# Expert bodies in another order with hinted jumps, and 20 weight rooms instead of 18

## The chip, the cores and the metric

The kernel runs on 1 core of one Trainium2 chip. The metric is the device time of one execution in microseconds; lower is better. TensorE is called PE below (its weight loads PEld), VectorE DVE, ScalarE ACT, GpSimd POOL, and SyncE SP.

## What is computed

A two-layer trunk over 256 latent tokens and 256 context tokens of width 1024: a layer with a convolution branch and a gating branch and a dense SwiGLU, then latent attention, and then the part that this case is about, a mixture of 8 experts of which each token takes 2:

```python
def _moe(h, router, w1, w3, w2):
    ...
    logits = (hf @ router).astype(jnp.float32)
    top_v, top_i = lax.top_k(logits, TOP_K)
    top_w = jax.nn.softmax(top_v, axis=-1)
    gates = jnp.sum(jax.nn.one_hot(top_i, N_EXPERTS, dtype=jnp.float32) * top_w[..., None], axis=-2).astype(h.dtype)
    y = jnp.zeros_like(hf)
    for e in range(N_EXPERTS):
        y = y + gates[:, e:e + 1] * _swiglu(hf, w1[e], w3[e], w2[e])
    return y.reshape(b, t, d)
```

All is float32. Expert width is 3584, so one expert has 3 x 1024 x 3584 weights, 44 MB, and the eight have 352 MB, which are read once.

## The kernel before

The first part (to about 768 us) runs the trunk up to the router. After it the kernel knows how many tokens each expert got. Tokens are handled in groups of 32, and an expert runs with 1, 2, 3 or 4 groups. This number is only known on the chip: line 1089 packs the eight numbers, two bits each (0 means one group, 2 means three), into one integer, which every engine reads into a register at line 1323. For each expert the program holds four bodies, one for each number of groups, and every engine branches to the one it needs:

```python
with tc.If(groups >= 2, preferred_fallthrough_block=True) as many:
    with tc.If(groups == 2, preferred_fallthrough_block=True) as three:
        body(3)
    with three.Else():
        body(4)
with many.Else():
    with tc.If(groups == 1, preferred_fallthrough_block=True) as two:
        body(2)
    with two.Else():
        body(1)
```

Code stands in the order of writing: the test for this expert, its bodies for 3, 4, 2 and 1 groups, then the test for the next expert. The block that stands right behind a test is reached without a jump; a body that is not the last one ends with a jump over those behind it.

A body (`expert`, line 1181) is seven steps j. In each, `up` (L1196) multiplies the gathered tokens with four rooms of weights, ACT and DVE form the SwiGLU (L1205, L1206), `turn` (L1212) transposes it, and `down` (L1225) multiplies it with two rooms, one step late. At the end `scale` (L1255) and `scatter` (L1266, L1270) add the result to the latents. Tokens are gathered for two experts at once: `hots` (L1113) makes a one-hot tile G, and `gather` (L1129, L1130) fills an operand tile xf, for the next pair at the end of the experts with odd number.

Weights come in pieces of 128 x 2048 floats, 1 MB, 42 to an expert, through a ring of 18 rooms: 6 from a pool of their own (`MORE`, tile names room), 4 and 8 that the trunk used before (roomsplit, raw). `ring.load()` (L172) is called when a room has been used and issues the load of the piece that is 18 pieces ahead; it stands on SP's queue and waits until PE has read the room. The order of instructions within PE, ACT and DVE is that of the code. The scratch tiles (line 265) come from a pool of six buffers that are handed out in turn.

Of the kernel before, what the change touches and what calls it, by code (L numbers as in the profile page):

```python
# [19 lines left out]
P = 128  # L20
# [18 lines left out]
MORE = 6  # L39
# [205 lines left out]
def trunk(ctx: ExitStack, tc, w, out, taps=None):  # L245
# [39 lines left out]
    right = ExitStack()  # L285
    xp = right.enter_context(tc.tile_pool(name="xp", bufs=1, side="right"))
# [86 lines left out]
    class Sum:  # L373


        def __init__(self, n):
            self.n, self.acc, self.last = n, None, None

        def square(self, ap):
            if self.acc is None:  # L380
                self.acc = small.tile([P, T], F32, tag="sum", name="sum", bufs=2)[:, : self.n]
                nc.scalar.activation(self.acc, ap, AF.Square)
            else:
                if self.last is not None:
                    nc.vector.tensor_add(self.acc, self.acc, self.last)
                self.last = scratch()[:, : self.n]
                nc.scalar.activation(self.last, ap, AF.Square)
# [84 lines left out]
    st = Sum(T)  # L472
# [23 lines left out]
    with tc.tile_pool(name="mix", bufs=1, side="right", reuse_waits="tile") as mix:  # L496
# [181 lines left out]
        st = Sum(T)  # L678
# [26 lines left out]
        var = Sum(T)  # L705
# [43 lines left out]
    with tc.tile_pool(name="ffn", bufs=1, side="right", reuse_waits="tile") as fp:  # L749
# [11 lines left out]
        st = Sum(T)  # L761
# [50 lines left out]
    with tc.tile_pool(name="latent", bufs=1, side="left", reuse_waits="tile") as lt:  # L812
        kvl = lt.tile([P, 2, T], F32, name="kvl")
        ql = lt.tile([P, 3, TX], F32, name="ql")
        skv, sq = Sum(T), Sum(TX)
# [182 lines left out]
    st = Sum(TX)  # L998
# [108 lines left out]
    with tc.tile_pool(name="exp", bufs=1, side="right", reuse_waits="tile") as ep:  # L1107
# [3 lines left out]
        def hots(p):  # L1111
            G = ep.tile([P, 2, 2, CAP], F32R, tag="G", name="G")
# [4 lines left out]
        def operand_room():  # L1117
            return ep.tile([P, KD, 2, CAP], F32, tag="xf", name="xf", bufs=2)

        def gather(p, ks, kind):  # L1120

            if p not in xfs:
                xfs[p] = operand_room()
# [57 lines left out]
        def expert(e, s):  # L1181
# [27 lines left out]
            def turn(h):  # L1209
# [3 lines left out]
                ht = ep.tile([P, 512], F32, tag="ht", name="ht", bufs=2)  # L1213
# [37 lines left out]
            def scale():  # L1251
                y = ep.tile([P, N_GROUPS, 2 * P], F32, tag="y", name="y")
                for b in range(nb):
                    n = min(2, s - 2 * b)
                    nc.vector.tensor_mul(y[:, 2 * b : 2 * b + n, :], state["y"][b][:, :n, :],  # L1255
                                         gate_row.unsqueeze(1).to_broadcast([P, n, 2 * P]))
                return y

            def scatter(y):
                back = state["back"]  # L1260
                accs = [bank("BC"[t % 2]) for t in range(4)]
                for t in range(2):
                    for g in range(s):
                        for q in range(4):
                            row = slice(32 * q, 32 * q + 32)
                            nc.tensor.matmul(accs[q][:, t * TX : (t + 1) * TX], back[row, g, t * P : (t + 1) * P], y[row, g, :],  # L1266
# [6 lines left out]
            for j in range(N_J):  # L1273
# [20 lines left out]
            y = scale()  # L1294
            if after:
                gather(after, range(4, KD), "A")
            scatter(y)
# [16 lines left out]

        hots(0)
        tokens(0, (1,))
# [36 lines left out]
        def overflow():  # L1353

            G = ep.tile([P, 2, 2, CAP], F32, tag="G", name="G")[:, 0]
            GT = ep.tile([P, N_GROUPS, TX], F32, tag="back", name="back")[:, 0, :]
            y = ep.tile([P, N_GROUPS, 2 * P], F32, tag="y", name="y").rearrange("p g n -> p (g n)")
            ht = ep.tile([P, 512], F32, tag="ht", name="ht", bufs=2)
# [191 lines left out]
```

## Time and profile before

| | |
|---|---|
| runs, us | 1744.45, 1745.65, 1749.63 (median 1745.65) |
| profiled execution: its time | 1745.33 us |
| profiled execution: its span | 1743.5 us |
[...]
| busy: PE, DVE, ACT | 1628.2, 510.4, 388.7 us |
| data moved | 470.40 MB |

The span is the time from the first to the last instruction of one profiled execution. Busy time of PE is the time in which at least one of its pipelined matmuls was under way. The profile's other views are: the chain of waits (from the last instruction back, at each step to what released it), the timeline (instructions in order of time, with the idle time before them and what ended it), the stretches (busy time of each engine, granted clock and share of the 16 DMA engines in a given window) and the waits (who waited for whom).

### The profile page before, as it was taken

How to read it: one execution, taken by the hardware profiler on the slowest of the kernel's cores; microseconds unless marked ns; L12 is line 12 of the kernel's file. 1: busy time of each engine (PE TensorE's matmuls, PEld its weight loads, DVE VectorE, ACT ScalarE, POOL GpSimd, SP SyncE). 2: the span in 40 equal slices, each digit the busy share in tenths (PEclk: the TensorE clock that was granted, in tenths of full speed). 3: DMA queues.
4: the chain of work that ended last, by engine and by line, in shares of the span. 5: the costliest groups of instructions: out<-in, count | busy, mean ns of one | idle time of the engine just before them, and what ended most of it. 6: DMA issues, size and time to landing. Idle time of an engine off the chain costs nothing.

```text
span 1743.5 us, 40718 instructions
## 1 busy us (share of the span) xinstructions
PE 1628.2 (93%) x18697; PEld 1109.3 (64%) x18697; DVE 510.4 (29%) x929; ACT 388.7 (22%) x724; POOL 23.1 (1%) x20
## 2 busy tenths in 40 slices
PE   8998999999999999999967799989999967998996
PEld 5676678888888787876533455555665533555654
DVE  3899763333433667720010000010010010100001
ACT  4343452222223355632000100000100001000101
POOL 0022000000000000000000000000000000000000
PEclk9999999999999999999988899999999987999998
DMA  9652562222222544689969999969979969999970
GB/s 379 225 233 73 242 242 97 94 88 97 91 79 97 200 187 176 232 325 354 394 247 421 419 419 351 298 250 367 399 295 379 377 259 420 419 419 418 418 287 28
DMA packets 67332, 470.40 MB, mean 270 GB/s; under 512 B 7456, under 2 KB 7840, under 8 KB 13088
## 3 DMA queue, kind: packets, MB, share of 16 engines
q1 hardware_dynamic: 67104, 467.13, 69.0%
q8 instruction: 171, 2.80, 0.7%
q14 instruction: 57, 0.47, 0.1%
HBM read 466.05 MB, written 1.05 MB: 268 GB/s over the span
## 4 chain that ended last, share of the span: by engine, by line
PE 83%; DMA 9%; DVE 3%; issue 3%; ACT 1%; SPq 0%; ACTq 0%; DVEq 0%
PE bankA L1196 28%; PE bankB L1225 13%; PE bankA L270 7%; PE bankA L271 7%; PE bankA L272 7%; DMA raw<-e 6%; PE bankB L271 3%; PE bankB L270 3%; PE bankB L272 3%; DVE cv L524 2%; PE bankC L339 2%; DMA room<-e 2%; PE bankC L1212 1%; DMA roomsplit<-e 1%; PE bankA L339 1%
## 5 line engine op out<-in xcount | busy, mean ns | idle before, releaser
L1206 DVE TENSOR_TENSOR scratch<-scratch,bankA 128x256 f32<-128x256 f32 (+1 forms) x98 | 31.9, 353 | 783.3 <-ACT scratch L1205 783.3
L1196 PE MATMUL bankA<-raw,xf 128*32 128x256 f32 x3888 | 231.5, 392 | 28.4 <-issue 16.9
L1196 PEld LDWEIGHTS bankA<-raw,xf 128*32 128x32 f32 x3888 | 130.3, 113 | 115.7 <-issue 32.3
L1196 PE MATMUL bankA<-room,xf 128*32 128x256 f32 x3264 | 190.1, 388 | 9.8 <-issue 4.9
L132 DVE TENSOR_TENSOR split<-raw,split 128x1024 fp32r<-128x1024 f32 (+4 forms) x121 | 139.9, 1158 | 113.3 <-ACT split L131 111.0
L1205 ACT ACTIVATE scratch<-bankA 128x256 f32<-128x256 f32 (+1 forms) x98 | 32.2, 330 | 597.5 <-PE bankA L1196 595.8
L131 ACT CAST split<-raw 128x1024 fp32r<-128x1024 f32 (+4 forms) x121 | 118.0, 980 | 199.5 <-PE bankA L272 121.3
L1196 PEld LDWEIGHTS bankA<-room,xf 128*32 128x32 f32 x3264 | 106.3, 112 | 85.0 <-issue 12.4
L1196 PE MATMUL bankA<-roomsplit,xf 128*32 128x256 f32 x2256 | 132.3, 392 | 23.9 <-issue 21.2
L270 PE MATMUL bankA<-hq,split 128*128 128x512 f32 (+1 forms) x380 | 148.7, 392 | 1.4 <-ACT hq L450 1.4
L271 PE MATMUL bankA<-hq,split 128*128 128x512 f32 (+1 forms) x380 | 148.2, 390 | 0.9 <-DVE hq L453 0.9
L272 PE MATMUL bankA<-hq,split 128*128 128x512 f32 (+1 forms) x380 | 147.3, 388 | 0.0
L1225 PE MATMUL bankB<-raw,ht 128*32 128x256 f32 x2288 | 135.2, 388 | 7.5 <-DMA raw<-e 5.5
L1196 PEld LDWEIGHTS bankA<-roomsplit,xf 128*32 128x32 f32 x2256 | 75.9, 113 | 77.0 <-issue 27.4
L1225 PEld LDWEIGHTS bankB<-raw,ht 128*32 128x32 f32 x2288 | 74.3, 112 | 61.3 <-DMA raw<-e 6.7
L1225 PE MATMUL bankB<-room,ht 128*32 128x256 f32 x1632 | 92.9, 382 | 6.1 <-DMA room<-e 4.9
L524 DVE SCALAR_TENSOR_TENSOR cv<-pad,prm,cv 128x512 f32<-128x512 f32 x106 | 86.0, 848 | 0.8
L270 PEld LDWEIGHTS bankA<-hq,split 128*128 128x128 f32 x380 | 71.6, 189 | 21.9 <-issue 3.4
L271 PEld LDWEIGHTS bankA<-hq,split 128*128 128x128 f32 x380 | 71.7, 189 | 16.2 <-DVE hq L453 1.4
L272 PEld LDWEIGHTS bankA<-hq,split 128*128 128x128 f32 x380 | 71.6, 188 | 14.5
L1225 PEld LDWEIGHTS bankB<-room,ht 128*32 128x32 f32 x1632 | 52.8, 110 | 42.8 <-DMA room<-e 3.6
L1214 ACT COPY ht<-bankC 128x384 f32<-128x384 f32 (+2 forms) x56 | 24.6, 439 | 242.3 <-PE bankC L1212 242.3
(403 smaller groups left out, 2028.3 us busy)
## 6 DMA issues: line engine op xcount, KB each, us to landing
raw<-e SPq DMA_DIRECT2D x146, 1024.0 KB, 10.4
room<-e SPq DMA_DIRECT2D x114, 1024.0 KB, 11.5
roomsplit<-e SPq DMA_DIRECT2D x72, 1024.0 KB, 9.4
raw<-ada SPq DMA_DIRECT2D x48, 1024.0 KB, 7.6
raw<-f SPq DMA_DIRECT2D x26, 1024.0 KB, 5.2
raw<-f SPq DMA_DIRECT2D x8, 896.0 KB, 4.7
raw<-win SPq DMA_DIRECT2D x6, 1024.0 KB, 7.7
raw<-wout SPq DMA_DIRECT2D x4, 1024.0 KB, 8.4
```

The lines of the kernel that those rows point to most:

```text
L131: self.nc.scalar.copy(wh[:, :size], raw)
L132: self.nc.vector.tensor_sub(wl[:, :size], raw, wh[:, :size].bitcast(F32))
L270: nc.tensor.matmul(acc, wh, ah, start=first, stop=False)
L271: nc.tensor.matmul(acc, wh, al, start=False, stop=False)
L272: nc.tensor.matmul(acc, wl, ah, start=False, stop=last)
L339: nc.tensor.matmul(acc[32 * q : 32 * q + 32, :], cs[:, 4 * h + q, :], wt[:, q, :], start=(h == 0), stop=(h == 1), tile_position=(0, 32 * q))
L524: nc.vector.scalar_tensor_tensor(out=o, in0=i, scalar=cw[:, m, j : j + 1], in1=o, op0=ALU.mult, op1=ALU.add)
L1196: nc.tensor.matmul(accs[g // 2][32 * q : 32 * q + 32, g % 2], xf[:, k, g * GROUP : (g + 1) * GROUP], piece[:, k - kk, :, q * P : (q + 1) * ...
L1205: nc.scalar.activation(part, acc[:, :n, 0, :], AF.Silu)
L1206: nc.vector.tensor_mul(part, part, acc[:, :n, 1, :])
L1214: nc.scalar.copy(ht[:, : s * P], tp[:, : s * P])
L1225: nc.tensor.matmul(state["y"][g // 2][32 * t : 32 * t + 32, g % 2], ht[:, g * P + f * GROUP : g * P + (f + 1) * GROUP], piece[:, f - ff, t ...
```

## The change

There are three parts.

The order of the bodies: the first test is now whether the expert has other than three groups, and the code stands in the order test, bodies for 1, 4, 2 and 3 groups, next test. A body for 1, 4 or 2 groups ends with a jump, that for 3 groups runs into the next test. At the start of each body, PE gets a hint instruction that names the next expert's first test and, from the packed number, whether it will jump (0, three groups) or not (1). One such hint, with a fixed direction, stands ahead of the first expert. Only PE has hints, and only the first test of each expert is named by one.

The rooms: `MORE` is 8 instead of 6, so the ring has 20 rooms.

The space for them: the operand tile xf exists once instead of twice; G, ht and y are taken from the scratch tiles, y as one or two tiles; G is made right ahead of the gather instead of in step 3; the row of final gains has a tile of its own; and the tiles in which squares are summed move from a pool that lives throughout to pools of the stages.

```diff
-MORE = 6
+MORE = 8
...
     right = ExitStack()
+    sums_of = right.enter_context(tc.tile_pool(name="sums", bufs=2, side="right"))
...
-                self.acc = small.tile([P, T], F32, tag="sum", name="sum", bufs=2)[:, : self.n]
+                self.acc = self.pool.tile([P, self.n], F32, tag=f"sum{self.n}", name="sum", bufs=1 if self.n < T else 2)
...
         def hots(p):
-            G = ep.tile([P, 2, 2, CAP], F32R, tag="G", name="G")
+            G = scratch(F32R).rearrange("p (t i s) -> p t i s", t=2, i=2)
...
         def operand_room():
-            return ep.tile([P, KD, 2, CAP], F32, tag="xf", name="xf", bufs=2)
+            return ep.tile([P, KD, 2, CAP], F32, tag="xf", name="xf")
...
-                ht = ep.tile([P, 512], F32, tag="ht", name="ht", bufs=2)
+                ht = scratch()
...
             def scale():
-                y = ep.tile([P, N_GROUPS, 2 * P], F32, tag="y", name="y")
-                for b in range(nb):
+                ys = [scratch().rearrange("p (g n) -> p g n", g=2) for _ in range(nb)]
+                for b, y in enumerate(ys):
...
-                if j == 3 and after:
-                    hots(after)
...
             if after:
+                hots(after)
                 gather(after, range(4), "A")
...
+        xfs[0] = operand_room()
         hots(0)
+        tc.mark_branch_hint_location("groups0", engines={mybir.EngineType.PE})
...
-            if e == N_EXP - 2:
-                fg_row = operand_room().rearrange("p k i s -> p (k i s)")[:, :D]
             if e % 2 and e + 1 < N_EXP:
-                xfs[e // 2 + 1] = operand_room()
+                xfs[e // 2 + 1] = xfs[0]
+            if e == N_EXP - 1:
+                fg_row = ep.tile([P, D], F32, name="fg_row")
...
                 with ordered():
+                    if e + 1 < N_EXP:
+                        tc.mark_branch_hint_location(f"groups{e + 1}", hint=(packed // 4 ** (e + 1)) % 4 != 2,
+                                                     engines={mybir.EngineType.PE})
                     expert(e, s)
 
-            with tc.If(groups >= 2, preferred_fallthrough_block=True) as many:
-                with tc.If(groups == 2, preferred_fallthrough_block=True) as three:
-                    body(3)
-                with three.Else():
-                    body(4)
-            with many.Else():
-                with tc.If(groups == 1, preferred_fallthrough_block=True) as two:
-                    body(2)
-                with two.Else():
+            with tc.If(groups != 2, preferred_fallthrough_block=True, label=f"groups{e}") as other:
+                with tc.If(groups == 0, preferred_fallthrough_block=True) as one:
                     body(1)
+                with one.Else():
+                    with tc.If(groups == 3, preferred_fallthrough_block=True) as four:
+                        body(4)
+                    with four.Else():
+                        body(2)
+            with other.Else():
+                body(3)
```

PE's order in the built program, at the entry to the first expert. Before, both tests are followed by the body for three groups (24 matmuls to a room, 8 to a group):

```order
L1323 TENSOR_LOAD classes
L1339 REGISTER_ALU
L1339 COMPARE_AND_BRANCH
L1340 REGISTER_ALU
L1340 COMPARE_AND_BRANCH
L1196 MATMUL bankA<-room_5418,xf 32x256 x24
L1196 MATMUL bankA<-room_5420,xf 32x256 x24
```

Now:

```order
L1322 TENSOR_LOAD classes
L1341 REGISTER_ALU
L1341 COMPARE_AND_BRANCH
L1342 REGISTER_ALU
L1342 COMPARE_AND_BRANCH
L1337 ISA
L1337 REGISTER_ALU
L1546 BRANCH_PREFETCH_HINT
L1195 MATMUL bankA<-room_5422,xf 32x256 x8
L1195 MATMUL bankA<-room_5424,xf 32x256 x8
```

The body for one group now follows the tests, with a hint and two register instructions at its start; the body for three groups has moved to the end.

PE's order where the first expert's last body ends and the second expert begins. Before, that last body is the one for one group, and the one for three groups follows the second expert's tests:

```order
L1266 MATMUL bankC<-y,back 128x256
L1345 UNCONDITIONAL_BRANCH
L1339 ISA
L1339 COMPARE_AND_BRANCH
L1340 REGISTER_ALU x2
L1340 COMPARE_AND_BRANCH
L1196 MATMUL bankA<-raw_5453,xf 32x256 x24
```

Now the last body is the one for three groups:

```order
L1264 MATMUL bankC<-scratch,back 128x256
L1341 UNCONDITIONAL_BRANCH
L1341 ISA
L1341 COMPARE_AND_BRANCH
L1342 REGISTER_ALU x2
L1342 COMPARE_AND_BRANCH
L1337 ISA
L1337 REGISTER_ALU
L1546 BRANCH_PREFETCH_HINT
L1195 MATMUL bankA<-room_5426,xf 32x256 x8
```

An expert with three groups now runs straight into a next expert with one group, as one with one group ran into one with three before. The branch at the end of the last body leads to the row behind it.

## Rows read from the trace of the kernel before

**Rows 1.** The page's head.
```profile
span 1743.5 us, 40718 instructions
```

**Rows 2.** Chain of waits, second to fourth expert: start us, us, what, with matmul records.
```profile
915.66 3.59 PE bankA L1196 x64
...
999.99 13.95 PE bankA L1196 x256
...
1161.68 10.50 PE bankA L1196 x192
1172.18 5.18 PE bankB L1225 x96
1177.36 0.48 PE bankC L1212 x3
```

**Rows 3.** Waits of SP's queue: line, releaser, us in total, times, longest.
```profile
SPq L172 <- PE bankA L1196: 343.6, 143, 13.6
```

**Rows 4.** Timeline of PE, first up of each expert: start, us, work, [idle before <-releaser].
```profile
768.58 10.57 PE L1196 MATMUL bankA<-room,xf 128*32 128x256 f32 x192 [0.69 <-issue]
903.88 5.03 PE L1196 MATMUL bankA<-raw,xf 128*32 128x256 f32 x64 [14.08 <-issue]
980.86 4.49 PE L1196 MATMUL bankA<-roomsplit,xf 128*32 128x256 f32 x39 [5.70 <-issue]
1145.62 1.07 PE L1196 MATMUL bankA<-room,xf 128*32 128x256 f32 x4 [3.17 <-issue]
1274.57 12.25 PE L1196 MATMUL bankA<-raw,xf 128*32 128x256 f32 x192 [2.81 <-issue]
1409.72 5.35 PE L1196 MATMUL bankA<-roomsplit,xf 128*32 128x256 f32 x48 [14.26 <-issue]
1480.73 10.57 PE L1196 MATMUL bankA<-room,xf 128*32 128x256 f32 x192
1605.33 0.23 PEld L1196 LDWEIGHTS bankA<-raw,xf 128*32 128x32 f32 x8 [5.78 <-issue]
1605.36 13.04 PE L1196 MATMUL bankA<-raw,xf 128*32 128x256 f32 x192 [5.41 <-DMA roomsplit<-e]
```

**Rows 5.** DMA queues from 889 to 904 us: packets, MB, share of 16 engines.
```profile
q8 instruction: 5, 0.08, 3.2%
```

**Rows 6.** Stretches: length, PE PEld DVE ACT POOL busy, PEclk, DMA share, GB/s.
```profile
1140.00:1160.00 20.00, 15.77 (x232) 8.57 (x226) 2.48 (x4) 0.00 (x0) 0.00 (x0) 0.83 0.42 155
1500.00:1520.00 20.00, 20.00 (x371) 11.89 (x365) 1.54 (x5) 1.80 (x5) 0.00 (x0) 1.00 1.01 419
1680.00:1700.00 20.00, 20.00 (x367) 11.91 (x363) 1.26 (x4) 1.80 (x5) 0.00 (x0) 1.00 0.36 134
```

**Rows 7.** The same in stretches of 5 us, first to second expert.
```profile
890.00:895.00 5.00, 0.00 (x0) 0.00 (x0) 1.98 (x4) 0.00 (x0) 0.00 (x0) 0.81 0.37 146
895.00:900.00 5.00, 0.00 (x0) 0.00 (x0) 0.00 (x0) 0.00 (x0) 0.00 (x0) 0.50 0.04 8
900.00:905.00 5.00, 1.12 (x12) 0.69 (x16) 0.00 (x0) 0.00 (x0) 0.00 (x0) 0.50 0.04 7
905.00:910.00 5.00, 4.16 (x57) 2.14 (x49) 0.29 (x1) 0.28 (x1) 0.00 (x0) 0.83 0.60 195
```

**Rows 8.** The same, fifth to sixth expert.
```profile
1395.00:1400.00 5.00, 0.47 (x8) 0.06 (x2) 2.48 (x4) 0.00 (x0) 0.00 (x0) 0.82 0.48 192
1400.00:1405.00 5.00, 0.00 (x0) 0.00 (x0) 0.00 (x0) 0.00 (x0) 0.00 (x0) 0.50 0.05 8
1405.00:1410.00 5.00, 0.28 (x4) 0.23 (x8) 0.00 (x0) 0.00 (x0) 0.00 (x0) 0.50 0.04 7
1410.00:1415.00 5.00, 5.00 (x52) 2.65 (x48) 0.00 (x0) 0.00 (x0) 0.00 (x0) 0.50 0.48 136
```

**Rows 9.** Instructions that use G: durations ns min/median/max, first and last start.
```profile
L1113 DVE TENSOR_TENSOR G<-cst,pos x4: 683/684/691, 756.9 to 1432.8; 128x512 fp32r<-128x512 f32 x4
```

More of the change, by code (lines that the diff above doesn't have):

```diff
@@ L373, in trunk, with __init__ @@
     class Sum:
-        def __init__(self, n):
-            self.n, self.acc, self.last = n, None, None
+        def __init__(self, n, pool):
+            self.n, self.pool, self.acc, self.last = n, pool, None, None
         def square(self, ap):
             if self.acc is None:
-                self.acc = small.tile([P, T], F32, tag="sum", name="sum", bufs=2)[:, : self.n]
+                self.acc = self.pool.tile([P, self.n], F32, tag=f"sum{self.n}", name="sum", bufs=1 if self.n < T else 2)
                 nc.scalar.activation(self.acc, ap, AF.Square)
@@ L471, in trunk @@
     warm(13)
-    st = Sum(T)
+    st = Sum(T, sums_of)
     for k in range(KD):
@@ L677, in trunk @@
         ready_for(AF.Sqrt, u[:, 3, :])
-        st = Sum(T)
+        st = Sum(T, sums_of)
         def mix_out(h):
@@ L704, in trunk @@
             nc.tensor.matmul(mean, mean_w, cv[:, m, :], start=(m == 0), stop=(m == 3))
-        var = Sum(T)
+        var = Sum(T, sums_of)
         for m in range(4):
@@ L759, in act @@
             return s
-        st = Sum(T)
+        st = Sum(T, sums_of)
         for t in range(3):
@@ L814, in trunk @@
         ql = lt.tile([P, 3, TX], F32, name="ql")
-        skv, sq = Sum(T), Sum(TX)
+        skv, sq = Sum(T, lt), Sum(TX, lt)
         for m, acc in outer([f"owkv{m}" for m in range(3)], hi, lo):
@@ L997, in trunk @@
     raw_lg = bank("C")
-    st = Sum(TX)
+    st = Sum(TX, rp)
     ready_for(AF.Sqrt, o)
@@ L1117, in operand_room @@
         def operand_room():
-            return ep.tile([P, KD, 2, CAP], F32, tag="xf", name="xf", bufs=2)
+            return ep.tile([P, KD, 2, CAP], F32, tag="xf", name="xf")
         def gather(p, ks, kind):
-            if p not in xfs:
-                xfs[p] = operand_room()
             for k in ks:
@@ L1251, in scale, with scatter @@
             def scale():
-                y = ep.tile([P, N_GROUPS, 2 * P], F32, tag="y", name="y")
-                for b in range(nb):
+                ys = [scratch().rearrange("p (g n) -> p g n", g=2) for _ in range(nb)]
+                for b, y in enumerate(ys):
                     n = min(2, s - 2 * b)
[L1255 to L1259, printed above, removed]
+                    nc.vector.tensor_mul(y[:, :n, :], state["y"][b][:, :n, :], gate_row.unsqueeze(1).to_broadcast([P, n, 2 * P]))
+                return ys
+            def scatter(ys):
                 back = state["back"]
@@ L1265, in scatter @@
                             row = slice(32 * q, 32 * q + 32)
-                            nc.tensor.matmul(accs[q][:, t * TX : (t + 1) * TX], back[row, g, t * P : (t + 1) * P], y[row, g, :],
+                            nc.tensor.matmul(accs[q][:, t * TX : (t + 1) * TX], back[row, g, t * P : (t + 1) * P], ys[g // 2][row, g % 2, :],
                                              start=(t == 0 and g == 0), stop=(t == 1 and g == s - 1), tile_position=(32 * q, 0))
@@ L1291, in expert @@
             if after:
+                hots(after)
                 gather(after, range(4), "A")
             down(N_J - 1, ht)
-            y = scale()
+            ys = scale()
             if after:
                 gather(after, range(4, KD), "A")
-            scatter(y)
+            scatter(ys)
         def final_norm():
@@ L1353, in overflow @@
         def overflow():
-            G = ep.tile([P, 2, 2, CAP], F32, tag="G", name="G")[:, 0]
+            G = scratch().rearrange("p (i t s) -> p i t s", i=2, t=2)[:, 0]
             GT = ep.tile([P, N_GROUPS, TX], F32, tag="back", name="back")[:, 0, :]
-            y = ep.tile([P, N_GROUPS, 2 * P], F32, tag="y", name="y").rearrange("p g n -> p (g n)")
-            ht = ep.tile([P, 512], F32, tag="ht", name="ht", bufs=2)
+            y, ht = ep.tile([P, KD, 2, CAP], F32, tag="xf", name="xf").rearrange("p k i s -> p (k i s)")[:, :D], scratch()
             rooms, row, xe = ring.rooms[: ROOMS], ring.rooms[ROOMS][:, :D], ring.rooms[ROOMS + 1][:, :D]
```

## Prediction

> **What bounds the kernel now.** I read the page's head first: the profiled execution spans 1743.5 us [rows 1]; its own time is 1745.33 us, 1.8 more, and the median of the three runs is 1745.65, so a sum made against the profile carries over unchanged. Then the chain of waits, from 768 us on, where the experts begin: each expert is an alternation of up, turn and down, and its number of groups can be read from the matmul records of one up, 64 per group: 64 records in 3.59 us, 192 in 10.50, 256 in 13.95 [rows 2]. Read so, the eight experts e0 to e7 run with 3, 1, 4, 3, 3, 1, 3, 3 groups. Each needs 42 rooms of 1 MB. Where the transfers are saturated they move 419 GB/s [rows 6], so a room takes 1.0486 MB / 0.419 = 2.50 us, and one j of six rooms 15.0 us. PE needs for the same j 10.50 + 5.18 + 0.48 = 16.2 us with three groups and more with four; with one group an up takes 3.59 us for four rooms, 0.9 each. So experts of 3 and 4 groups are bound by PE, and the ring of 18 rooms stands full ahead of them; e1 and e5, with one group, eat the ring up and are then bound by the transfers. The queue confirms it: the loads of line 172 wait 343.6 us for a room that PE frees [rows 3].
>
> Third, the timeline at the change from one expert to the next. I name the gap in PE between the last scatter and the first up, and how many jumps PE makes there by the old order of the bodies (test, 3, 4, 2, 1 groups, next test): e0-e1 three jumps (out of body 3, to the second test, to body 1), 14.08 us; e1-e2 one (to body 4), 5.70; e2-e3 one, 3.17; e3-e4 one, 2.81; e4-e5 three, 14.26; e5-e6 none, and the up starts with no gap at all; e6-e7 one, 5.41, which PE's weight loads put to "issue" [rows 4]. The chain lays that last wait to a DMA, but the room had landed long before: the transfers run ahead of PE there and end by 1690 [rows 6]. So a jump has a price, and rows give it: one jump 2.8 to 3.2 us where the transfers pause, 5.4 to 5.7 where they are saturated, and each further jump in a row (14.2 - 3.0) / 2 = **5.6 us** (the first is cheaper because scatter's matmuls are still queued ahead of it). During a gap the code queue moves 16 KB packets, 5 of them between 889 and 904 us [rows 5], so the wait is for code.
>
> [...]
>
> **Two of the gaps stop the transfers too.** In e0-e1 PE frees no room for 14 us. The ring is full, and the DMA share falls to 0.37, 0.04, 0.04, 0.60 [rows 7]: idle (0.63 + 0.96 + 0.96 + 0.40) x 5 = 14.8 us. In e4-e5 likewise: (0.52 + 0.95 + 0.96 + 0.52) x 5 = 14.8 us [rows 8]. As e1 and e5 end when their last room lands, these 15 us each are on the path.
>
> **The change, transition by transition.** The new order of the bodies is test, 1, 4, 2, 3 groups, next test. A jump to body 3 now carries a hint from the body before; all other jumps carry none.
>
> - Into e0: before, body 3 follows the test (a gap of 0.69 us [rows 4]); now a hinted jump. Bounds 0 and 5.6; I take +0.5, close to the 0.69 of the entry without a jump, since the hint stands at the program's start.
> - e0-e1 and e4-e5: no jump any more (body 3, next test, body 1 stand in a row, as e5-e6 does now with no gap). The transfers still pause until PE has freed its first room (0.9 us of a one-group up) and the queue has issued: about 1 us. That leaves -13.8 for each.
> - Two more rooms: at the ends of e0 and e4 the ring is full, so two more rooms of e1 and e5 lie ready, 2 x 2.50 = -5.0 each. The DMA share is 0.42 around e2-e3 [rows 6], so there is time to fill them. In the other experts they are worth nothing, as PE is the bound.
> - e1-e2: two jumps without a hint instead of one (body 1 to the next test, test to body 4). The second costs 5.6, or 8.2 if saturated transfers add the same 2.6 as they do to a single jump (5.41 - 2.81). I take +8.2, since the transfers are saturated there.
> - e2-e3: one jump as before, then a hinted one straight behind it. Bounds 0 and 5.6; the hint has only the few instructions of the test to work in. I take +3.
> - e3-e4: only a hinted jump, reached by falling through. 2.81 + 1.7 goes, 0.5 stays for the tests: -4.0. Bounds -4.5 and 0.
> - e5-e6: before no jump; now an unhinted one (5.5, saturated), a hinted one right behind (0 to 8.2, I take 5), and the slow first up (2.5): +13, bounds +8 and +16.2. PE is the bound from there to the end, so all of it counts.
> - e6-e7: only a hinted jump: 5.41 + 2.5 - 0.5 = -7.4, bounds -7.9 and 0.
>
> Everything else I cost at nothing. G is now made right ahead of its use: 0.68 us on DVE [rows 9], while PE does a down; in e1 and e5, where PE waits for rooms, this is free, and if the cover were gone it would be 0.7 us three times. One operand tile instead of two: its next contents are written after the last up that reads it. Shared scratch: six buffers, and each comes round again after three uses of the pair h, ht, when its reader is long done. The sums move to other pools ahead of the experts with their orders unchanged. Two more loads stand on SP's queue behind all weights of the trunk. ACT, DVE and SP jump without hints too: ACT and DVE have the next expert's first up (10.5 us and more before a three- or four-group body) as cover, SP the loads that are already queued. The three instructions for a hint at a body's start are hidden behind scatter where PE falls through.
>
> Sum, in the order of the experts: +0.5 - 18.8 + 8.2 + 3 - 4.0 - 18.8 + 13 - 7.4 = **-24.3**, so 1745.33 - 24.3 = **1721 us**.
>
> [...] The rows show code coming in 16 KB packets, and PE standing still for 14 us while a handful of them move [rows 5]. [...]
>
> **The rivals.**
>
> 1. The hints do nothing (the change doesn't do all it says). Each jump to body 3 then costs what an unhinted one does: +5.6 into e0, +5.6 at e2-e3, 0 at e3-e4 and e6-e7, +16.2 at e5-e6. Sum: 5.6 - 18.8 + 8.2 + 5.6 + 0 - 18.8 + 16.2 + 0 = -2.0, or 1743. For it: no row shows a hint at work. Against: only that the program names branch and direction well ahead. Chance 0.16.
> 2. The hints work even right behind another jump: nothing into e0, nothing at e2-e3, +8 at e5-e6, and 5.6 instead of 8.2 at e1-e2. Sum: 0 - 18.8 + 5.6 + 0 - 4.0 - 18.8 + 8 - 7.4 = -35.4, or 1710. Chance 0.08.
> 3. The rooms bring nothing, or the hinted jumps out of a fall-through hide only in part (the test may stand early in its code block): up to 10 us of the gain go, 1729 to 1739. Against the first: the idle transfers in rows 7 and 8 say that the ring was full. Chance 0.12.
> 4. Slower: a hint at a body's start makes PE fetch the far block at once and drop the code that it needs next, so that each of the seven bodies with a hint stalls at its start. At a price p the sum is -24.3 + 7p; it is slower than before by over 0.3% once p passes 4.2 us. At the 5.6 of a chained jump it is +14.9, or 1760. Nothing in the trace speaks for it, and the price of a jump is above the point, so it can't be excluded. Chance 0.06.
>
> The forecast itself, 1713 to 1729, has 0.58.
>
> **How the numbers follow.** About 0.3%, 5.2 us, is what a measurement here can tell from no change. Faster by more (below 1740.4): 0.58 + 0.08 + 0.12, and a third of rival 1 (0.06), 0.84. Same: the rest of rival 1, 0.10. Slower: 0.06. Range 1708 to 1743: it leaves out half of rival 2 (0.04), half of rival 1 (0.08) and rival 4 (0.06).
>
> **What would show it.** Right: the two gaps of 14 us gone, the first up of e1 and e5 within 1 us of the scatter, and the DMA share near 1 through both; e1 and e5 done about 19 us sooner after the scatter before them; gaps of under 1 us at e3-e4 and e6-e7; gaps of some 12 to 14 us at e1-e2, 6 at e2-e3 and 10 at e5-e6. Wrong: gaps of 3 to 5 us still at e3-e4 and e6-e7 (the hints do nothing), gaps at a body's start behind its first instructions (rival 4), or a pause of the transfers of over 3 us at e0-e1 (some other engine or the queue jumps late).

## The result, and the profile of the changed kernel

The changed kernel takes 1718.22 us, the median of four runs (1716.95 to 1720.21), against 1746.78 us for the kernel before (four runs, 1744.45 to 1749.63): a ratio of 0.9837, with an interval of 0.9818 to 0.9855. The forecast was 1721 us. The profiled execution is the longest of the four, 1720.21 us; its span, from the head of the page of after, answers to [rows 1]:

```profile
span 1718.4 us, 40666 instructions
```

The timeline of PE in the changed kernel, first up of each expert, answers to [rows 4] (start, us, work, idle time before it in brackets; up is line 1195 now). A new line begins where the room's name changes or where PE waited inside the up; behind such a wait the second piece has a bracket too.

```profile
769.24 12.25 PE L1195 MATMUL bankA<-room,xf 128*32 128x256 f32 x192 [1.03 <-issue]
...
891.94 3.66 PE L1195 MATMUL bankA<-room,xf 128*32 128x256 f32 x64
...
970.36 1.46 PE L1195 MATMUL bankA<-room,xf 128*32 128x256 f32 x9 [13.50 <-issue]
975.49 16.48 PE L1195 MATMUL bankA<-room,xf 128*32 128x256 f32 x247 [3.67 <-issue]
...
1141.74 7.09 PE L1195 MATMUL bankA<-room,xf 128*32 128x256 f32 x96 [5.96 <-issue]
1148.64 5.37 PE L1195 MATMUL bankA<-raw,xf 128*32 128x256 f32 x96
...
1265.09 10.57 PE L1195 MATMUL bankA<-raw,xf 128*32 128x256 f32 x192
...
1384.25 2.80 PE L1195 MATMUL bankA<-raw,xf 128*32 128x256 f32 x48
...
1460.05 4.08 PE L1195 MATMUL bankA<-raw,xf 128*32 128x256 f32 x48 [11.28 <-issue]
...
1581.35 3.22 PE L1195 MATMUL bankA<-roomsplit,xf 128*32 128x256 f32 x54
1585.83 5.12 PE L1195 MATMUL bankA<-roomsplit,xf 128*32 128x256 f32 x89 [1.26 <-issue]
```

There are no brackets at 891.94 (e1) and 1384.25 (e5), where [rows 4] had 14.08 and 14.26, and none at 1265.09 (e4) and 1581.35 (e7), where the jump is hinted. At the ends of the one-group bodies, which now jump twice, the brackets are 13.50 and 11.28.

With the two long gaps the pauses of the transfers are gone. Stretches of 5 us of the changed kernel, first to second expert and fifth to sixth (length, PE, PEld, DVE, ACT, POOL busy, granted clock, DMA share, GB/s), answer to [rows 7, 8]:

```profile
880.00:885.00 5.00, 4.38 (x76) 2.42 (x71) 0.00 (x0) 0.48 (x1) 0.00 (x0) 1.00 0.98 400
885.00:890.00 5.00, 4.62 (x82) 2.97 (x78) 1.02 (x2) 0.00 (x0) 0.00 (x0) 1.00 0.95 364
890.00:895.00 5.00, 5.00 (x95) 3.44 (x91) 2.48 (x4) 0.00 (x0) 0.00 (x0) 1.00 0.90 283
895.00:900.00 5.00, 4.16 (x77) 2.27 (x73) 0.29 (x1) 0.54 (x2) 0.00 (x0) 1.00 0.97 395
...
1380.00:1385.00 5.00, 4.62 (x80) 3.41 (x76) 2.00 (x4) 0.00 (x0) 0.00 (x0) 1.00 0.96 359
1385.00:1390.00 5.00, 4.07 (x76) 2.18 (x72) 1.79 (x4) 0.55 (x2) 0.00 (x0) 1.00 0.88 316
```

The idle share over the four stretches at e0-e1 is (0.02 + 0.05 + 0.10 + 0.03) x 5 = 1.0 us, and (0.04 + 0.12) x 5 = 0.8 us at e4-e5, where before it was 14.8 us each. The queue's longest wait for an up fell from 13.6 us [rows 3] to 7.9:

```profile
SPq L172 <- PE bankA L1195: 341.7, 148, 7.9
```

To compare kernels I take for each expert the time from the last scatter matmul of the one before it to its own last one, from PE's records in one profiled execution of each kernel. The gap, the first up and the wait for rooms of an expert are all within it. "Trunk" is the time from the span's start to the end of PE's work ahead of e0's gap.

| kernel | trunk | e0 | e1 | e2 | e3 | e4 | e5 | e6 | e7 |
|---|---|---|---|---|---|---|---|---|---|
| before | 767.9 | 121.9 | 85.4 | 167.3 | 129.3 | 123.7 | 85.3 | 119.2 | 130.3 |
| after | 768.2 | 123.8 | 64.9 | 178.9 | 129.4 | 119.2 | 64.5 | 132.7 | 124.3 |
| again (after once more) | 766.4 | 123.8 | 64.7 | 176.8 | 130.4 | 119.2 | 64.9 | 133.1 | 124.3 |
| nohint | 767.3 | 131.8 | 65.3 | 176.2 | 134.8 | 127.0 | 64.3 | 134.2 | 129.5 |
| rooms18 | 767.7 | 123.8 | 71.5 | 177.2 | 130.1 | 119.2 | 69.0 | 133.4 | 124.7 |
| old20 | 767.9 | 121.6 | 80.7 | 167.2 | 129.8 | 124.5 | 82.0 | 119.2 | 130.2 |
| order18 | 765.5 | 126.3 | 71.0 | 176.4 | 134.4 | 126.7 | 71.0 | 134.7 | 129.6 |
| wrong | 767.2 | 122.1 | 65.3 | 178.7 | 131.8 | 124.1 | 64.4 | 134.7 | 130.1 |
| lateh | 766.2 | 121.7 | 64.5 | 178.3 | 128.9 | 119.2 | 64.4 | 132.5 | 124.4 |
| rooms21 | 762.5 | 122.1 | 63.8 | 177.1 | 130.3 | 119.2 | 63.6 | 132.6 | 124.8 |
| moved20 | 765.3 | 123.8 | 64.7 | 177.3 | 130.6 | 119.2 | 64.7 | 132.6 | 124.5 |
| rooms21g | 763.0 | 123.8 | 64.5 | 178.7 | 129.7 | 119.2 | 62.4 | 132.6 | 124.7 |
| hintab | 763.3 | 123.8 | 61.6 | 172.3 | 129.0 | 119.2 | 63.7 | 136.0 | 134.9 |
| hintb | 763.6 | 123.9 | 64.4 | 176.4 | 129.0 | 119.2 | 61.6 | 134.5 | 124.8 |

After minus before, worked out ahead of rounding: trunk +0.3, e0 +1.9, e1 -20.5, e2 +11.6, e3 +0.1, e4 -4.6, e5 -20.9, e6 +13.5, e7 -6.0, and the tail behind e7 -0.5, in all -25.1, as the spans differ (1743.5 and 1718.4). The medians differ by 28.6; the profile of after is of its longest run, and again, the same kernel, has a span of 1716.4.

The trace also has the time that each of PE's branches took (line, queue, operation, count, then ns as least, median and most, and the start in us). At e4, in after, nohint and wrong:

```profile
L1341 PEldq COMPARE_BRANCH  x1: 378/378/378, 1263.9 to 1263.9; - x1
...
L1337 PEldq COMPARE_BRANCH  x1: 3576/3576/3576, 1274.2 to 1274.2; - x1
...
L1341 PEldq COMPARE_BRANCH  x1: 3937/3937/3937, 1263.9 to 1263.9; - x1
```

The hinted jump took 0.38 us, the same jump without a hint 3.58, and with a hint of the wrong direction 3.94. At e3 and e6, where an unhinted jump stands ahead of it, the jump to body 3 took, in after and nohint:

```profile
L1341 PEldq COMPARE_BRANCH  x1: 2919/2919/2919, 1138.3 to 1138.3; - x1
...
L1337 PEldq COMPARE_BRANCH  x1: 4541/4541/4541, 1143.2 to 1143.2; - x1
...
L1341 PEldq COMPARE_BRANCH  x1: 5582/5582/5582, 1453.9 to 1453.9; - x1
...
L1337 PEldq COMPARE_BRANCH  x1: 7273/7273/7273, 1472.0 to 1472.0; - x1
```

There the hint saved 1.6 and 1.7 us of the jump and left the rest.

### The profile page after: what moved, and what is told of

It reads as the page before. It is cut to its first block, busy times and chain, and to the rows that moved or that the text cites. A ratio compares the mean times of both kernels' runs of the same rounds, so it can differ in the third digit from the quotient of the medians.

```text
span 1718.4 us, 40666 instructions
## 1 busy us (share of the span) xinstructions
PE 1621.3 (94%) x18697; PEld 1106.1 (64%) x18697; DVE 510.5 (30%) x929; ACT 389.3 (23%) x724; POOL 23.1 (1%) x20
## 4 chain that ended last, share of the span: by engine, by line
PE 87%; DMA 5%; DVE 4%; issue 3%; ACT 1%; SPq 0%; ACTq 0%; DVEq 0%
PE bankA L1195 29%; PE bankB L1224 14%; PE bankA L270 7%; PE bankA L271 7%; PE bankA L272 7%; PE bankB L271 3%; PE bankB L270 3%; PE bankB L272 3%; DMA room<-e 2%; DVE cv L525 2%; PE bankC L340 2%; PE bankC L1211 1%; DMA roomsplit<-e 1%; PE bankB L1264 1%; DMA raw<-e 1%
## 5 line engine op out<-in xcount | busy, mean ns | idle before, releaser
L1195 PE MATMUL bankA<-room,xf 128*32 128x256 f32 x3648 | 212.9, 392 | 31.4 <-issue 24.2
L1195 PE MATMUL bankA<-raw,xf 128*32 128x256 f32 x3888 | 222.8, 384 | 18.6 <-issue 11.3
L1195 PEld LDWEIGHTS bankA<-room,xf 128*32 128x32 f32 x3648 | 121.7, 113 | 114.7 <-issue 34.2
L1224 PE MATMUL bankB<-room,scratch 128*32 128x256 f32 x2080 | 119.2, 384 | 4.5 <-DMA room<-e 3.1
L1195 PE MATMUL bankA<-roomsplit,xf 128*32 128x256 f32 x1872 | 107.6, 382 | 3.4 <-DMA roomsplit<-e 1.9
L1224 PEld LDWEIGHTS bankB<-room,scratch 128*32 128x32 f32 x2080 | 67.4, 111 | 52.1 <-DMA room<-e 3.2
L1224 PE MATMUL bankB<-raw,scratch 128*32 128x256 f32 x1664 | 96.6, 384 | 2.3 <-ACT scratch L1213 1.2
L1195 PEld LDWEIGHTS bankA<-roomsplit,xf 128*32 128x32 f32 x1872 | 60.4, 110 | 44.8 <-issue 3.8
L271 PEld LDWEIGHTS bankA<-hq,split 128*128 128x128 f32 x380 | 71.7, 189 | 16.3 <-DVE hq L454 1.4
L1224 PEld LDWEIGHTS bankB<-raw,scratch 128*32 128x32 f32 x1664 | 54.0, 111 | 40.0 <-ACT scratch L1213 1.7
L1213 ACT COPY scratch<-bankC 128x384 f32<-128x384 f32 (+2 forms) x56 | 24.6, 440 | 232.2 <-PE bankC L1211 232.0
```

The source lines that it names most:

```text
L271: nc.tensor.matmul(acc, wh, al, start=False, stop=False)
L1195: nc.tensor.matmul(accs[g // 2][32 * q : 32 * q + 32, g % 2], xf[:, k, g * GROUP : (g + 1) * GROUP], piece[:, k - kk, :, q * P : (q + 1) * ...
L1213: nc.scalar.copy(ht[:, : s * P], tp[:, : s * P])
L1224: nc.tensor.matmul(state["y"][g // 2][32 * t : 32 * t + 32, g % 2], ht[:, g * P + f * GROUP : g * P + (f + 1) * GROUP], piece[:, f - ff, t ...
```

## The experiments

The theory is that of the prediction: the new order takes two 14-us gaps off the path and puts jumps elsewhere; the hints make the new jumps cheap; two more rooms save their transfers in e1 and e5. The rival asks whether the order and the rooms alone do it.

**nohint**: hints out, everything else as changed.

```diff
-        tc.mark_branch_hint_location("groups0", engines={mybir.EngineType.PE})
...
-                    if e + 1 < N_EXP:
-                        tc.mark_branch_hint_location(f"groups{e + 1}", hint=(packed // 4 ** (e + 1)) % 4 != 2,
-                                                     engines={mybir.EngineType.PE})
```

> The changed kernel without any hint. Theory (a hint brings the code of the far block ahead of a jump that is reached by falling through, and in part behind an unhinted jump): gaps of about 3 us at e3-e4 and 5 us at e6-e7 come back, with slower first ups behind them (+4.5 and +6 together with the gap), 3 to 6 us into e0, 0 to 8 more at e2-e3 and e5-e6. 1733 to 1745. Rival (hints do nothing, the order of the bodies does all): 1718, no gap at e3-e4 and e6-e7.

Measured 1744.40 us, ratio 0.999 (0.9977 to 1.0002) to the kernel before. Order and rooms without hints gain nothing: what they save in e1 and e5 the other jumps take. The timeline of nohint, first ups of e0, e2, e3, e4 and e7:

```profile
775.20 13.36 PE L1195 MATMUL bankA<-room,xf 128*32 128x256 f32 x192 [7.89 <-issue]
...
977.42 3.17 PE L1195 MATMUL bankA<-room,xf 128*32 128x256 f32 x25 [13.01 <-issue]
982.61 14.23 PE L1195 MATMUL bankA<-room,xf 128*32 128x256 f32 x231 [2.03 <-issue]
...
1147.90 1.03 PE L1195 MATMUL bankA<-room,xf 128*32 128x256 f32 x3 [7.26 <-issue]
1151.20 7.70 PE L1195 MATMUL bankA<-room,xf 128*32 128x256 f32 x91 [2.27 <-issue]
...
1277.90 1.06 PE L1195 MATMUL bankA<-raw,xf 128*32 128x256 f32 x14 [2.46 <-issue]
1281.06 12.56 PE L1195 MATMUL bankA<-raw,xf 128*32 128x256 f32 x178 [2.10 <-issue]
...
1605.60 10.30 PE L1195 MATMUL bankA<-roomsplit,xf 128*32 128x256 f32 x144 [4.66 <-issue]
```

Against the changed kernel's lines 1.03, 5.96, none and none, the hints are worth, by the table, 8.0 us at e0, 5.4 at e3, 7.8 at e4, 1.6 at e6 and 5.2 at e7, less 2.7 lost at e2 (0.6 against again); the medians differ by 26 us. The two kernels differ in the hints alone, and at e4 the gap is 2.46 us without the hint and none with it.

**rooms18**: the changed kernel with `MORE = 6` instead of 8, so 18 rooms.

> The changed kernel with 18 rooms instead of 20. Theory (e1 and e5 end when their last room lands, and two more rooms lie ready at their start): each of the two lasts 5.0 us longer, nothing else moves, 1728. Rival (the rooms change nothing, as PE bounds the experts): 1718. Second rival (the rooms explain also the 1.7 and 2.1 us that e1 and e5 gained beyond the forecast): 1732.

Measured 1729.08 us, ratio 0.9897 (0.9873 to 0.9921). The two rooms are worth 10.9 us by the medians, 6.6 in e1 and 4.6 in e5; without them e1 and e5 are 13.9 and 16.3 us shorter than before.

**old20**: the old order of the bodies, no hints, 20 rooms.

```diff
-            with tc.If(groups != 2, preferred_fallthrough_block=True, label=f"groups{e}") as other:
...
+            with tc.If(groups >= 2, preferred_fallthrough_block=True) as many:
...
```

> The old order of the bodies, no hints, but 20 rooms and the shared tiles. Theory: the gaps of 14 us stay, the transfers still pause for some 15 us in each, but two more rooms are filled in that time, so -5.0 us at e1 and at e5 against the kernel before: 1737. Rival (rooms worth nothing without the order): 1747. The shared tiles by themselves cost nothing in either.

Measured 1737.10 us, ratio 0.9949 (0.9929 to 0.9968): the rooms, the shared tiles and the one operand tile without the rest are worth 7.7 us, 4.7 in e1 and 3.4 in e5. The shared tiles and the one operand tile, which were costed at nothing, did cost nothing that shows.

**wrong**: hints with the direction reversed; the one into e0 stays as it is.

```diff
-                        tc.mark_branch_hint_location(f"groups{e + 1}", hint=(packed // 4 ** (e + 1)) % 4 != 2,
+                        tc.mark_branch_hint_location(f"groups{e + 1}", hint=(packed // 4 ** (e + 1)) % 4 == 2,
```

> The changed kernel with the direction of each hint turned round: it says jump where the code falls through (other than three groups next) and no jump where three groups are next. Theory (a hint decides which code is fetched): gaps at e3-e4 and e6-e7 as without hints, and new gaps of 3 to 6 us at e0-e1 and e4-e5, where the code behind the test was not fetched; 1740 to 1756, slower than without hints. Rival 1 (hints do nothing): 1718. Rival 2 (a wrong hint costs nothing, since the code in sequence is fetched as well): as without hints.

Measured 1732.16 us, ratio 0.9913 (0.9888 to 0.9938): a miss. Against nohint it gained 9.7 us at e0, whose hint was still right, which I had left out of the expectation. Where a jump to body 3 comes, the gaps are near those of no hint (7.52, 3.18, 13.08 and 4.69 us at e3, e4, e6 and e7, against 7.26, 2.46, 12.75 and 4.66). But e3 and e4 are 3.0 and 2.9 us shorter than in nohint, as the waits of 2.27 and 2.10 us inside their first ups are gone; with e0 this is most of what wrong gained. Whether the hints did that or the place of the code, which they shift, no run separates. Where no jump came, the up behind a hint that said "taken" waited, 2.54 us in e1 and 0.81 in e5; nohint has no such wait there. The timeline of wrong, first ups of e1, e4, e5 and e7:

```profile
889.22 2.35 PE L1195 MATMUL bankA<-room,xf 128*32 128x256 f32 x37
894.11 1.92 PE L1195 MATMUL bankA<-room,xf 128*32 128x256 f32 x27 [2.54 <-issue]
...
1268.31 12.25 PE L1195 MATMUL bankA<-raw,xf 128*32 128x256 f32 x192 [3.18 <-issue]
...
1393.60 0.63 PE L1195 MATMUL bankA<-roomsplit,xf 128*32 128x256 f32 x5 [0.81 <-issue]
...
1593.01 4.91 PE L1195 MATMUL bankA<-roomsplit,xf 128*32 128x256 f32 x54 [4.69 <-issue]
```

The waits of 2.54 and 0.81 us cost nothing here, as e1 and e5 wait for rooms anyway: 65.3 and 64.4 us, as in nohint.

**order18**: nohint with 18 rooms, so the order of the bodies alone.

> The changed kernel without its hints and with 18 rooms: the new order of the bodies alone (with the one operand tile). Theory (order, rooms and hints add up, and the rooms are worth what they were worth beside the hints, 1729.1 - 1718.2 = 10.9 us): 1744.4 + 10.9 = 1755 us, slower than the kernel before by some 10 us, with gaps of 7 to 8 us into e0, 13 at e1-e2, 7 at e2-e3, 2 to 5 at e3-e4 and e6-e7, 12 to 13 at e5-e6. Rival (without hints the chip waits for code anyway and the rooms fill in those gaps, so they hide nothing): 1744.

Measured 1749.91 us, ratio 1.0024 (1.0010 to 1.0038): the order alone (with the shared tiles) makes the kernel slower, by some 4 to 5 us, half of the 10 expected. In e1 and e5 the two rooms are worth 5.7 and 6.7 us (order18 against nohint), as the theory has it; but the unhinted entry into e0 took 126.3 us here and 131.8 in nohint (gaps of 3.54 and 7.89), and the two traces show where. The branch took 3.32 us in order18 and 4.48 in nohint, and nohint then waited another 3.2 us ahead of its first matmul. The transfers differ as well; a stretch of order18, then the same of nohint:

```profile
765.00:770.00 5.00, 1.46 (x16) 0.85 (x18) 0.36 (x2) 1.13 (x1) 0.00 (x0) 0.89 0.03 10
...
765.00:770.00 5.00, 1.27 (x9) 0.82 (x8) 0.36 (x2) 2.71 (x4) 0.00 (x0) 1.00 0.97 397
```

With 18 rooms the weights had stopped coming (DMA share 0.03), with 20 they were still coming (0.97). The branch was dearer where the transfers ran, 4.48 us against 3.32, as the prediction's two prices for a jump have it; why nohint waited a second time, the runs don't tell.

**lateh**: the hint of a body stands ahead of its last down, not at its start.

```diff
+            if e + 1 < N_EXP:
+                tc.mark_branch_hint_location(f"groups{e + 1}", hint=(packed // 4 ** (e + 1)) % 4 != 2,
+                                             engines={mybir.EngineType.PE})
             down(N_J - 1, ht)
```

> The changed kernel with each body's hint standing just ahead of the last down instead of at the body's start, so some 10 us ahead of the jump with three groups instead of some 125; the hint into e0 is left as it is. Theory (a hint needs only a few us of lead, about what one unhinted jump costs): 1718 us, with gaps of under 1 us at e3-e4 and e6-e7 as in the changed kernel. Rival (the lead is too short, or the hint takes part of the code fetch that the body itself needs there): gaps of 2 to 5 us back at e3-e4 and e6-e7, 1722 to 1730.

Measured 1717.05 us, ratio 0.9853 (0.9837 to 0.9869): the same as the changed kernel, with no gap at e4 and e7. The trace has the hint for e7 at 1564.5 us and the test that it names at 1574.2: a lead of some 10 us was enough. First up of e2 in lateh, whose body has no hint at its start:

```profile
965.48 1.89 PE L1195 MATMUL bankA<-room,xf 128*32 128x256 f32 x11 [13.06 <-issue]
970.97 15.94 PE L1195 MATMUL bankA<-room,xf 128*32 128x256 f32 x245 [3.60 <-issue]
```

**rooms21**, **moved20** and **rooms21g**: a 21st room, paid for by three small tiles put into memory that is free by then (moved20 has these moves with 20 rooms); rooms21g also gathers all ahead of the last down in one-group bodies.

```diff
-MORE = 8
+MORE = 9
...
-        gate_row = ep.tile([P, 2 * P], F32, name="gate_row")
+        gate_row = cs.rearrange("p k n -> p (k n)")
...
-            ex = mo.tile([P, 2, N_EXP], F32, tag="ex", name="ex")
+            ex = gate
...
-                fg_row = ep.tile([P, D], F32, name="fg_row")
+                fg_row = xfs[0].rearrange("p k i s -> p (k i s)")[:, D:]
```

In rooms21g besides:

```diff
-                gather(after, range(4), "A")
+                gather(after, range(KD if s == 1 else 4), "A")
```

> The changed kernel with a 21st room, bought by putting three small tiles into memory that is free by then. Theory (in e1 and e5 every room that lies ready saves its transfer of 2.5 us, in all other experts none): 2 x 2.5 = 5 us less than the changed kernel, 1713 us; the one-group experts take 62.4 and 61.9 us from scatter to scatter instead of 64.9 and 64.4. Rival (the last two rooms filled all the idle time there was): 1718.

> As rooms21, and in one-group bodies the whole gather for the next pair of experts stands ahead of the last down instead of half of it behind. Theory (e1 and e5 end when their last room lands, so what PE does behind the last down is on the path and what it does ahead of it is hidden in the wait for that room): two half gathers of some 1.3 us less, 1710.5 us. Rival (the gather delays the last down by as much, or the wait is no longer there with 21 rooms): the same as rooms21.

> The kernel of the run rooms21 with 20 rooms instead of 21: the changed kernel with only the three small tiles moved into memory that is free by then. In the run rooms21 the two one-group experts together were only 2.0 us shorter than in the changed kernel, but the trunk ended 4 to 6 us sooner (at 773.9 us, and at 774.2 to 774.5 in the three other kernels with 21 rooms, against 776.8 to 779.6 in all kernels with 18 or 20). Theory (the moves of the small tiles shorten the trunk, the room is worth 2 us): the trunk ends at 774 to 775 us, time 1713 us. Rival (the trunk's end goes with the 21st room, which shifts the addresses of other tiles or starts one more load): the trunk ends at 777 to 780 us, time 1718 us.

rooms21 took 1711.27 us, ratio 0.9815 (0.9802 to 0.9829); rooms21g 1713.07, 0.9819 (0.9806 to 0.9832); moved20 1716.75, 0.9832 (0.9819 to 0.9845). rooms21 is the fastest kernel here, but not by its theory. In the three kernels with 21 rooms and the old place of the gather (rooms21, hintab, hintb) e1 takes 63.2 us on average and e5 63.0, in the four with 20 rooms (after, again, lateh, moved20) 64.7 and 64.6: the room is worth 1.4 and 1.6 us, not 2.5 each. (The three with 21 rooms differ by up to 2.8 us among themselves, in one profile of each, so this is rough.) With 20 rooms the transfers had only 1.0 and 0.8 us of idle time left there to fill. A 21st room doesn't take all of that either, as two stretches of rooms21 at e4-e5 show:

```profile
1370.00:1375.00 5.00, 4.62 (x80) 3.41 (x76) 1.36 (x3) 0.00 (x0) 0.00 (x0) 1.00 0.95 316
1375.00:1380.00 5.00, 4.07 (x72) 2.18 (x76) 2.44 (x5) 0.43 (x2) 0.00 (x0) 1.00 0.92 334
```

The pause is (0.05 + 0.08) x 5 = 0.65 us. The rest of the gain is in the trunk: 762.5 to 763.6 us in all four kernels with 21 rooms, 765.3 to 768.2 in the ten others. (The expectation of moved20 counts the same moments from a start some 11 us earlier.) moved20 has 765.3, at the edge of those without the moves, and its time lies nearer the 1718 of the rival: the shorter trunk goes with the 21st room rather than with the moves. By what it does so is not settled. The gather ahead of the last down brought nothing in sum (e1 +0.8, e5 -1.2 against rooms21).

**hintab** and **hintb**: in one-group bodies of rooms21 a hint for the inner test of the next expert, behind the first hint (hintab) or in its place (hintb).

```diff
+                    if e + 1 < N_EXP and s == 1:
+                        tc.mark_branch_hint_location(f"one{e + 1}", hint=(packed // 4 ** (e + 1)) % 2 == 0,
+                                                     engines={mybir.EngineType.PE})
...
-                with tc.If(groups == 0, preferred_fallthrough_block=True) as one:
+                with tc.If(groups == 0, preferred_fallthrough_block=True, label=f"one{e}") as one:
```

> The kernel of the run rooms21 (21 rooms) and, in one-group bodies alone, a second hint behind the first: it names the inner test (one group or not) of the next expert, and says taken where the next expert has two or four groups. So at e1-e2 the jump at the inner test, which goes to body 4 and carries no hint so far, has one. Theory (an unhinted second jump costs 5 to 8 us there, and a hint behind another jump is worth 1.6 to 5.4 as it was at e5-e6 and e2-e3): 2 to 5 us less at e1-e2, nothing elsewhere, so 1706 to 1709 us. Rival 1 (two hints share one place, and the second takes away the first even where it says not taken): e1-e2 gains as much, but e5-e6 loses its hint, some 1.6 us. Rival 2 (the wait at e1-e2 is for the exit jump and for the code behind body 4's first block, not for the inner test): no gain, 1711.

> As hintab, but one-group bodies carry only the second hint (the inner test), not the first. Theory: e1-e2 as in hintab, and e5-e6, where the next expert has three groups, costs what it did without hints, 15.0 instead of 13.4 us: 1.6 us more than hintab where that keeps both hints, the same where rival 1 of hintab holds.

hintab took 1717.16 us, ratio 0.984 (0.982 to 0.986), and hintb 1711.91, 0.9815 (0.9797 to 0.9833). The timeline of hintab, first ups of e2 and e7:

```profile
960.53 16.69 PE L1195 MATMUL bankA<-room,xf 128*32 128x256 f32 x256 [11.79 <-issue]
...
1572.48 2.62 PE L1195 MATMUL bankA<-room,xf 128*32 128x256 f32 x29 [3.60 <-DMA roomsplit<-e]
1578.02 12.09 PE L1195 MATMUL bankA<-room,xf 128*32 128x256 f32 x163 [2.92 <-issue]
```

At e2 hintab gained 4.8 us against rooms21, the size that the theory had. e6 lost 3.4, more than rival 1 said, and e7 lost 10.1, which nothing foretold: body 3 of e6 hints the jump to e7 as ever, and the gap of 3.60 us came all the same. (The profile puts it to a DMA; the wait of PE's weight loads there, 3.97 us, it puts to "issue", as at e7 in [rows 4].) hintb gained only 0.8 us at e2, though it has the same inner hint, so its theory missed; it has no loss at e7, and its e6 lost 1.8, the price of the missing hint. The branches tell more. The jump at the inner test of e2 took 6.78 us in rooms21, 5.29 in hintab and 5.04 in hintb, so the inner hint goes with 1.5 to 1.7 us less in both. The rest of hintab's gain is a wait of some 4 us inside the first up (4.03 in rooms21, 3.80 in hintb) that hintab has not; that the inner hint took it away is not shown. In hintab the jump to body 3 of e6 took 7.38 us, as long as in hintb (7.36), which has no hint for it, against 5.60 in rooms21: the first of the two hints gained nothing there, as rival 1 said. The one into e7 took 4.98 us, where after has 0.37. That two hints get in each other's way fits both; how, the runs don't tell.

**again**: the changed kernel beside these two.

> The changed kernel once more, unaltered, beside the two runs of this call: 1718 us, so that 21 rooms and the second hint are compared with it on the same chip; gaps within 1 us of those of its first profile.

Measured 1719.30 us, ratio 0.9858 (0.9835 to 0.9882), and e2 2.1 us shorter and e3 1.0 longer than in its first profile: that much of a gap with unhinted jumps is chance.

## Why the prediction was right

The mechanism held: the two gaps of 14 us and the pauses of the transfers went, the two rooms paid in e1 and e5, a hinted jump reached by falling through took 0.37 to 0.40 us, and without hints it all came to nothing. That the sum is so close is in part luck, as single terms were off by up to 3.4 us and cancel.

By its own terms, forecast against the table (after minus before):

| step | forecast | measured |
|---|---|---|
| into e0 | +0.5 | +1.9 |
| e1: gap gone, two rooms | -18.8 | -20.5 |
| e1-e2: one more unhinted jump | +8.2 | +11.6 (again: +9.5) |
| e2-e3: unhinted, then hinted jump | +3 | +0.1 (again: +1.1) |
| e3-e4: hinted jump | -4.0 | -4.6 |
| e5: gap gone, two rooms | -18.8 | -20.9 |
| e5-e6: unhinted, then hinted jump | +13 | +13.5 |
| e6-e7: hinted jump | -7.4 | -6.0 |
| sum of the terms | -24.3 | -24.9 |

The 1.7 and 2.5 us that the forecast counts at e3-e4, e5-e6 and e6-e7 for a slow first up are differences of [rows 4]: 12.25 us behind a gap of 2.81 and 13.04 behind one of 5.41, against 10.57 without a gap. In the gap of e0-e1 the granted clock was 0.50 [rows 7].

**e1 and e5** were two terms each, and rooms18 takes them apart: the gap -13.9 and -16.3 (forecast -13.8), the rooms -6.6 and -4.6 (-5.0). order18, which has 18 rooms as well, has -14.3 in both, so the gaps are worth some 14 us and the 2 us more in e5 of rooms18 may be the scatter of one profile.

**The hinted jumps out of a fall-through** did what was forecast: no gap, and at e3-e4 a first up of 10.57 us, as short as one without a gap. At e6-e7 a wait of 1.26 us came inside the first up, which took 12.42 us. That is the partial hiding of rival 3, worth 1.4 us.

**Hints behind an unhinted jump** hid only part: the jumps took 2.92 and 5.58 us, without the hint 4.54 and 7.27. At e2-e3 the gap of 5.96 is the 6 forecast; what I missed is the wait inside the first up. Before:

```profile
1145.62 1.07 PE L1196 MATMUL bankA<-room,xf 128*32 128x256 f32 x4 [3.17 <-issue]
1147.76 12.87 PE L1196 MATMUL bankA<-room,xf 128*32 128x256 f32 x188 [1.06 <-issue]
```

The gap grew by 2.8 us and the first up, without that wait, shortened by 2.7, from 15.0 to 12.3. The prediction's reason for +3, that the hint has only the few instructions of the test to work in, is not what the trace has: the hint ran at 970.2 us, the test it names at 1138.3. What went with the poorer hiding is the unhinted jump between the two. At e5-e6 the gap was 11.28 where 10 was forecast.

**e1-e2 was under-sized.** The second jump was priced right: the gap grew by 13.50 - 5.70 = 7.8 us. Left out was what follows: nine matmuls, 3.67 us more of waiting, in which one packet came on the code queue (q8, 0.02 MB from 971.9 to 975.5 us), and then a longer stretch at the lower clock. Such a wait stood there before too, but it was shorter:

```profile
986.59 8.58 PE L1196 MATMUL bankA<-roomsplit,xf 128*32 128x256 f32 x153 [1.25 <-issue]
```

The first up, waits included, grew from 17.8 to 21.6 us. Stretches of the changed kernel there:

```profile
965.00:970.00 5.00, 0.00 (x0) 0.00 (x0) 0.00 (x0) 0.00 (x0) 0.00 (x0) 0.50 1.01 408
970.00:975.00 5.00, 1.46 (x9) 0.58 (x10) 0.00 (x0) 0.00 (x0) 0.00 (x0) 0.50 1.01 418
975.00:980.00 5.00, 4.51 (x44) 2.59 (x47) 0.00 (x0) 0.00 (x0) 0.00 (x0) 0.50 1.02 421
```

The granted clock is 0.50 through all three. The step that failed is "the second costs 5.6, or 8.2": it priced the gap alone, and the up behind it grew by 3.8 us as well. The 5.6 itself was too high as well for a jump with paused transfers: the three branches of e0-e1 before took 5.82, 4.85 and 4.36 us in the trace, and the first began 1.7 us ahead of the end of scatter, which hid that much of it. The sum took the 8.2 instead, so little hung on this.

**Into e0**, 1.7 of the 1.9 us are not the jump. The gap is 1.03 us against 0.69, but the first up took 12.25 us instead of 10.57 because PE was at a lower clock, 0.84 and 0.68 against 1.00 in wrong: stretches of the changed kernel, then of wrong, which has the same entry.

```profile
765.00:770.00 5.00, 2.93 (x25) 2.17 (x27) 0.36 (x2) 2.95 (x5) 0.00 (x0) 0.84 0.96 395
770.00:775.00 5.00, 5.00 (x68) 3.36 (x64) 0.00 (x0) 0.00 (x0) 0.00 (x0) 0.68 0.18 34
```

```profile
765.00:770.00 5.00, 2.94 (x44) 2.04 (x47) 0.36 (x2) 2.52 (x4) 0.00 (x0) 1.00 0.92 378
770.00:775.00 5.00, 5.00 (x100) 3.64 (x96) 0.00 (x0) 0.00 (x0) 0.00 (x0) 1.00 0.61 195
```

e0 took 121.7 to 122.1 us in three kernels with this entry and 123.8 to 123.9 in the others; what decides between the two, the runs don't tell. The bound of 5.6 us for this place was too low: without a hint it cost 4.4 (order18) and 9.9 us (nohint).

**The rivals.** Rival 1 was the sum without hints, 1743 us, and nohint took 1744.4: the sum held, its condition did not, and its terms only in part (e0 cost 9.9 instead of 5.6, e4 3.3 instead of nothing). Rival 2, hints that work as well behind another jump, falls with the gaps of 5.96 and 11.28. Rival 3 falls with rooms18, but for the 1.4 us. Rival 4's sign, a gap at a body's start behind its first instructions, is there at e2 (3.67 us after nine matmuls). But the bodies of e1, e3, e4 and e5 have none, e2 has such a wait without hints too (2.03 us after 25 matmuls in nohint), and lateh, with no hint at the start of its bodies, has 3.60: the hint at the body's start is not the cause, and rival 4 falls. Why this wait is longer with hints (3.67 us in after, 3.36 in again) than without, no run shows. A wait at a false hint is seen only in wrong, 2.54 and 0.81 us. The forecast of 1721 was 3 us high. The two mis-sized terms around e2 are +3.4 and -2.9 and cancel to 0.5, and e1 and e5 (-1.7 and -2.1) cancel against e0 and e7 (+1.4 each): that is luck.

## What to carry to other kernels

Count the taken jumps on the way from one body to the next, read from the trace how long each branch took, and look whether the long wait of one engine also lets another resource, here the weight transfers, run dry: here two such places cost some 14 us each. The hints gained 5.2 to 8.0 us where the hinted jump was the only one on the way (e0, e4, e7) and 1.6 and 5.4 us behind an unhinted one (e6, e3); a lead of 10 us was enough (lateh). Reordering code without hints moved the waits here and gained nothing (order18, nohint), so measure the parts apart.

## What the runs showed of the hardware

- A taken jump over other bodies, without a hint, took PE 3.3 to 4.9 us where the transfers paused (order18 e0, the second and third of e0-e1 before) and 6.0 to 7.3 us where they were saturated (e2, e6 and e7 of nohint). The same jump with a hint, reached by falling through, took 0.37 to 0.40 us (after e0, e4, e7); behind an unhinted jump, 2.9 and 5.6 us (after e3, e6).
- The hinted jumps into e4 and e7 left no gap on PE, with first ups of 10.57 and 12.42 us; without a hint they left gaps of 2.46 and 4.66 us, with first ups of 15.72 and 12.89 (after, nohint). A lead of 10 us (lateh) did as well as one of over 100.
- PE waited twice at six places: behind a taken jump PE ran 3 to 59 matmuls of an up and then waited again, 0.28 to 3.67 us (e2, e6, e7 of after; e2, e3, e4 of nohint). Other first ups behind a jump have no such wait (e3, e4 of after).
- Behind a hint that said "taken" for a jump that wasn't taken PE waited 2.54 and 0.81 us inside the up that did follow (wrong, e1 and e5; no such wait in nohint).
- Two hints set one behind the other gained 4.8 us at one place and lost 13.5 at two others (hintab). Why, these runs don't settle.
- An unhinted jump into e0 cost 4.4 us in one kernel (order18) and 9.9 in another with the same code around it and two rooms more (nohint). With two rooms more the weights were still coming from 765 to 770 us (DMA share 0.97 against 0.03).
